# A two-layer decoder trunk on one core: weight-sum transfers tied to weight units, joined first-chunk scores, head squares summed on ScalarE, separate scrap blocks

## The chip, the cores and the metric

The kernel runs as one program on 1 core of one Trainium2 chip. The metric is the device time of one execution in microseconds (us), lower is better. TensorE (PE) multiplies matrices, VectorE (DVE) and ScalarE (ACT) work on whole tiles of 128 partitions, GpSimd (POOL) does small elementwise work and issues its own transfers, SyncE (SP) issues the other transfers.

## The reference

The input `x` is 512 tokens of 1024 numbers, float32. Two layers, each with RMS norm, one wide projection, a mixer, a gated output projection and a residual:

```python
for layer in range(DEPTH):
    h = rms_norm(x, norm_w[layer])
    y = even_layer(h, ...) if layer % 2 == 0 else hgrn2_layer(h, ...)
    x = x + y.astype(x.dtype)
```

Layer 0 splits the projected columns in two. mLSTM takes 4 heads of 128: a short convolution, then a matrix memory over chunks of 128 tokens, then `rms_norm` per head and two gates. NSA takes 8 query heads of 64 in 2 groups: q and the selected and window keys get an RMS norm per head and a partial rotation,

```python
qh = partial_rope(rms_norm(heads(q, NSA_HEADS), q_norm), pos) * (d ** -0.5)
ks_h = partial_rope(rms_norm(heads(ks, G), k_norm[1]), pos)
kw_h = partial_rope(rms_norm(heads(kw, G), k_norm[2]), pos)
```

and then come three branches of attention: over compressed blocks, over selected blocks and over a window. With 512 tokens all 8 blocks are selected and the window covers all earlier tokens, so the last two are both causal softmax attention, each with its own keys and values. Layer 1 (HGRN2) is a gated linear recurrence of 8 heads, again with `rms_norm` per head before its gate and its output projection.

## The kernel before, in words

**Products.** A float32 operand is split in a high part (`whi`, `h0h`) of TensorE's fast float32 format and the rest (`wlo`, `h0l`), and a product is three: high by high, low by high, high by low. The dense projections are groups of 96 such products of 512 columns (8 blocks of 128 inputs, 3 products, 4 banks of PSUM). The groups of layer 0 are cg, nq, nkv, nz, mq, mk, mv, mo, mz and the output o00, o01; those of layer 1 are t0 to t3 with two paired groups p0, p1 between them, and o10, o11.

**Weight units.** A group's weights come in 4 units. SP loads `raw`, ACT copies it to `whi`, DVE subtracts to get `wlo` (`cvt_w`, l. 739). `Group.convert` (l. 771) does this for a unit of the next group while the present one multiplies. There are 4 buffers each of `whi` and `wlo`.

**Weight sums.** The paired groups multiply sums of weight blocks. `sums` (in `build`) makes them in DRAM: 16 transfers issued by POOL, 12 from the weights (`wt<-in_wall_dram`) and 4 between the sums themselves (`wt<-wt`), some of them adding to their target, 1 MB each. `Adds.put` (l. 580) issues one; the strand `presums` releases number n when the planned TensorE work has passed 95 + 10.5 n us (`PS`, l. 30). The sums are first loaded for layer 1 (`raw<-wt`).

**The order of the work.** All instructions are recorded through one helper, so the profile shows them all at L408 and they are told apart by the tile names. Strands of work (Python generators) are run in turn and recorded; then `Plan.flush` (l. 392) puts every engine's instructions in an order by its own list of costs and dependences (`Plan.edges`, l. 220). Each engine then executes its list in that order and waits where an input is missing. So an edit at one place also changes the order at others.

**Head norms.** `prep_q(i)` and `prep_k(i)`, i = 0 to 3, take the projected q (8 heads of 64) and keys (4 of 64) of 128 tokens: ACT squares the whole tile into `sq`, DVE sums each head (`qss`, `kss`), POOL computes the inverse root (`qrs`, `krs`: a `TENSOR_SCALAR` and a power) and multiplies the norm's weight in (`qk<-qk,qnB`), DVE multiplies (`x<-qk,krs`) and rotates, TensorE turns the tile (`tp<-cs,x`), and ACT and DVE split it into `q` and `kd`. The mLSTM and HGRN2 head norms square one head of 128 at a time on ACT with a running sum (`accum_out`) and write the squares themselves to a scrap tile `hj` that nobody reads.

**Scores.** `nsa_a` runs 16 units (2 groups, 2 pairs of heads, 2 heads, 2 branches), each over 4 query tiles i. A unit's tile i has 128 (i+1) keys: two products of that width (high and low keys, `sc<-kd,q`), then DVE masks and takes the extreme (`nm`), ACT exponentiates into `PP` with a running sum (`sm`), DVE scales. `nsa_b` turns `PP` on TensorE (`tp<-cs,PP`) and multiplies it with the values.

Of the kernel before, what the change touches and what calls it, by code (L numbers as in the profile page):

```python
# [28 lines left out]
HBN = 4  # L29
PS = 95000.0, 10500.0  # L30
D = 1024
NT = 4
# [132 lines left out]
class Plan:  # L165
# [54 lines left out]
    def edges(self):  # L220
        for o in self.ops:
# [25 lines left out]
            if o.after is not None:  # L247
                o.pred.setdefault(o.after, 0.0)
        for a, b in zip(self.ops, self.ops[1:]):
# [323 lines left out]
class Adds:  # L573
# [3 lines left out]
    def __init__(self, plan, flow, eng):  # L577
        self.plan, self.flow, self.eng = plan, flow, eng

    def put(self, out, src, add):  # L580
        ns = 2000.0 + 128 * free_size(out) * 4 / (50.0 if add else 100.0)
        k = {"_ns": ns, "_after": next(o for o in reversed(self.plan.ops) if o.eng == "T")}
        if add:
            k["accum_op"] = OP.add
        self.flow.work("P", 1000.0)
        self.plan.add("P", self.eng.dma_start, (out, src), k, 1000.0)


# [27 lines left out]
def build(tc, I, out):  # L616
# [6 lines left out]
    with ExitStack() as ctx:  # L623
# [135 lines left out]
        class Group:  # L759
# [11 lines left out]
            def convert(self, i):  # L771
                k = self.qs[i]
                self.fetch(i + 1)
                nw = pcc("mhn", k, 2) if self.name[:2] == "o0" and k < 4 else None
                self.w[k] = cvt_w(self.raw.pop(k), self.C, nw)

            def mms(self, p, j, k):
# [152 lines left out]
        def sums(q, n):  # L930

            a, b = f"r{2 * q}", f"r{2 * q + 1}"
            t1, t2, t3, t4 = (wt[q][:, 2048 * i:2048 * (i + 1)] for i in range(4))
            steps = [(t3, wblock(b, 0), 0), (t2, wblock(a, 0), 0), (t3, wblock(b, 1), 1), (t4, wblock(a, 1), 0),
                     (t1, wblock(a, 0), 0), (t2, t3, 1), (t1, wblock(b, 0), 1), (t4, t2, 1)]
            AQ.put(*steps[n])

        A1 = {}
# [8 lines left out]
        with ExitStack() as c0:  # L947
# [3 lines left out]
            def s_t(name, shape, bufs=2, dt=F32):  # L951
                return sp.tile(shape, dt, name=name, tag=name, bufs=bufs)
# [3 lines left out]
            def hb(n):  # L956
                return lambda: big[0] >= n
# [246 lines left out]
            def turn(x2):  # L1204
# [3 lines left out]
                return cut(p, (4, 128))  # L1208

            def prep_q(i):  # L1210
                yield hb(2)
                x = qk[i][:, :8, :]
                ts_ = slice(128 * i, 128 * (i + 1))
                sq = b_t("sq", (8, 64))
                A.activation(sq, x, AF.Square)
                P.tensor_tensor(x, x, cust(qnB, [[0, 8], [1, 64]]), op=OP.mult)
                ss = s_t("qss", [128, 8])
                V.tensor_reduce(ss, sq, axis=AX.X, op=OP.add)
                b_end()
                rq = s_t("qrs", [128, 8])  # L1220
# [18 lines left out]
            def prep_k(i):  # L1239
                yield hb(2)  # L1240
                x = qk[i][:, 8:, :]
                ts_ = slice(128 * i, 128 * (i + 1))
                sq = b_t("sq", (4, 64))
                A.activation(sq, x, AF.Square)
                P.tensor_tensor(x.rearrange("p (a b) c -> p a b c", a=2), x.rearrange("p (a b) c -> p a b c", a=2),
                                cust(knB, [[64, 2], [0, 2], [1, 64]], 64), op=OP.mult)
                ss = s_t("kss4", [128, 4])
                V.tensor_reduce(ss, sq, axis=AX.X, op=OP.add)
                b_end()
                rk = s_t("krs4", [128, 4])  # L1250
# [55 lines left out]

            def nsa_a():
                yield [E("q%d" % i) for i in range(4)] + [E("k%d" % i) for i in range(4)] + [E("gt")]
                for u, (g, pr, br, hh) in enumerate(UN):
                    hg = 4 * g + 2 * pr + hh  # L1310
                    yield [hb(1), lambda u=u: ndone[0] >= u - 1, SCS]
                    pp = b_t("PP", (1280,))
                    nm = s_t("nm", [128, 4], 3)
                    sm = s_t("sm", [128, 4], 3)
                    for i in range(NT):
                        n = 128 * (i + 1)
                        yield SCS
                        s = sc_t()
                        for c in range(2):
                            T.matmul(s[:, :n], q2[g][:, hh, pr, 128 * i:128 * (i + 1)], kd[g][:, c, br, :n],  # L1320
                                     start=c == 0, stop=c == 1)
                        V.tensor_tensor_reduce(s[:, :n], s[:, :n], cz[:, 512 - n:], 1.0, -NEG, op0=OP.add, op1=OP.min,
                                               accum_out=nm[:, i:i + 1])
                        A.activation(pp[:, OFF[i]:OFF[i] + n], s[:, :n], AF.Exp, bias=nm[:, i:i + 1], scale=-1.0,
                                     accum_out=sm[:, i:i + 1])
                    V.reciprocal(sm, sm)
                    V.tensor_tensor(sm, sm, cust(gt, [[24, 4]], 3 * hg + 1 + br), op=OP.mult)
                    for i in range(NT):
                        sl = slice(OFF[i], OFF[i] + 128 * (i + 1))
                        V.tensor_scalar(pp[:, sl], pp[:, sl], sm[:, i:i + 1], None, op0=OP.mult)  # L1330
                    PPs[u] = pp
                    fl.mark(E("A%d" % u))
                    if u % 8 == 7:
                        u_end(1 + u // 8)
# [3 lines left out]
            def nsa_b():  # L1338
                pts = []
                yp = None  # L1340
                for u, (g, pr, br, hh) in enumerate(UN):
                    yield [E("A%d" % u), hb(1)]
                    pp = PPs.pop(u)
                    ptl = b_t("PT", (1280,))
                    m = []
                    for kbs, o in (((0,), 0), ((1,), 512), ((2, 3), 896)):
# [3 lines left out]
                        for kb in kbs:  # L1350
                            for i in range(kb, NT):
                                T.transpose(tp[:, c:c + 128], pp[:, OFF[i] + 128 * kb:OFF[i] + 128 * (kb + 1)], idf)
                                c += 128
# [133 lines left out]
            def m_tok(t):  # L1487
# [216 lines left out]

            def presums():

                for n in range(16):
                    yield lambda: fl.pe >= PS[0] + PS[1] * n
                    sums(n % 2, n // 2)

            fl.cur.t = 0.0
            fl.add(presums(), 0)
            fl.add(dense0(), 9)
# [4 lines left out]
        with ExitStack() as c1:  # L1718
# [60 lines left out]
            def hgrn(h):  # L1779
# [339 lines left out]
```

## Time and profile before

| | |
|---|---|
| median of 3 executions | 621.58 us (619.12 to 622.77) |
| the profiled execution | 619.54 us, its span 617.8 us |
| mean granted TensorE clock of the profiled execution | 0.997 |
| instructions | 11670 |

The profiled execution is the one that all rows below come from. The span is the time from its first to its last instruction; 1.7 us lie around it. "Busy" rows give the sum of the durations on an engine, and TensorE's products overlap, so its share of 99% counts the time in which at least one is in flight. The distance from one product's start to the next one's start is the better measure of what it costs.

### The profile page before, as it was taken

What the parts mean: (1) busy time and instruction counts of PE and PEld (TensorE: products, weight loads), DVE (VectorE), ACT (ScalarE), POOL (GpSimd) and SP (SyncE); (2) the same over time, 40 slices, a digit from 0 to 9 for tenths busy, and PEclk for the clock granted to TensorE, in tenths of its full rate; (3) what the DMA queues carried; (4) which work ended last, traced back from release to release, by engine and by line L of the source; (5) the groups of instructions that cost most, each with busy time, mean ns of one, the idle gap of its engine ahead of it and who ended that gap; (6) DMA issues with size and microseconds to landing.
All of it is one profiled execution on the core that took longest, in us unless ns stands there. A gap on an engine that the chain in (4) does not pass through costs nothing.

```text
span 617.8 us, 11670 instructions
## 1 busy us (share of the span) xinstructions
PE 609.2 (99%) x4498; PEld 492.0 (80%) x4498; DVE 463.9 (75%) x988; ACT 326.4 (53%) x778; POOL 104.5 (17%) x131
## 2 busy tenths in 40 slices
PE   8999998999999999999999999999999999999997
PEld 8877886877777777888888887788877877788886
DVE  5888989988899875656746669997688798986441
ACT  7554433675676765273534757447527375565410
POOL 1424252031100000063003111023000100122100
PEclk9998999999999999999999999999999999999999
DMA  8823137679994004016244424473222215473111
GB/s 293 278 117 103 51 103 256 203 164 342 247 203 138 0 2 147 7 46 228 77 162 136 154 85 138 118 240 121 69 72 69 70 34 173 138 282 128 35 69 68
DMA packets 23526, 82.90 MB, mean 134 GB/s; under 512 B 3376, under 2 KB 4272, under 8 KB 20656
## 3 DMA queue, kind: packets, MB, share of 16 engines
q1 hardware_dynamic: 21168, 65.39, 32.2%
q0 software_dynamic: 2304, 16.78, 10.3%
q8 instruction: 35, 0.57, 0.4%
q14 instruction: 19, 0.16, 0.1%
HBM read 77.96 MB, written 20.97 MB: 160 GB/s over the span
## 4 chain that ended last, share of the span: by engine, by line
PE 92%; DVE 3%; DMA 1%; issue 1%; POOL 1%; ACT 1%; SPq 0%; ACTq 0%; DVEq 0%
PE mm L408 35%; PE mx L408 17%; PE my L408 15%; PE sc L408 8%; PE tp L408 5%; PE ac L408 5%; PE tq L408 5%; PE sd L408 2%; DMA raw<-in_wall_dram 1%; DVE wlo L408 1%; DVE HB L408 0%; DVE AL L408 0%; POOL krs L408 0%; ACT whi L408 0%; DVE x L408 0%
## 5 line engine op out<-in xcount | busy, mean ns | idle before, releaser
L408 ACT ACTIVATE whi<-raw 128x512 fp32r<-128x512 f32 (+1 forms) x184 | 105.0, 614 | 76.2 <-PE my L408 29.5
L408 DVE TENSOR_TENSOR wlo<-raw,whi 128x1024 fp32r<-128x1024 f32 (+1 forms) x96 | 114.7, 1202 | 20.4 <-ACT whi L408 20.1
L408 PE MATMUL mm<-whi,h0h 128*128 128x512 f32 (+1 forms) x168 | 68.2, 407 | 0.0
L408 PE MATMUL mm<-whi,h0l 128*128 128x512 f32 (+1 forms) x168 | 67.9, 405 | 0.0
L408 PE MATMUL mm<-wlo,h0h 128*128 128x512 f32 (+1 forms) x168 | 67.4, 405 | 0.0
L408 ACT ACTIVATE PP<-sc,nm 128x128 f32<-128x128 f32 (+2 forms) x64 | 33.7, 527 | 26.0 <-DVE nm L408 22.9
L408 DVE CUSTOM_DVE_ANT_0 sc<-sc,cz 128x128 f32<-128x128 f32 (+2 forms) x64 | 31.4, 502 | 11.7 <-PE sc L408 9.1
L408 PE MATMUL mm<-h0h,whi 128*128 128x512 f32 x96 | 39.5, 411 | 0.0
L408 PE MATMUL mm<-h0h,wlo 128*128 128x512 f32 x96 | 38.1, 397 | 0.6 <-DVE wlo L408 0.6
L408 PE MATMUL mm<-h0l,whi 128*128 128x512 f32 x96 | 38.6, 402 | 0.0
L408 PEld LDWEIGHTS mm<-whi,h0l 128*128 128x128 f32 x168 | 32.1, 192 | 5.8 <-issue 0.2
L408 PEld LDWEIGHTS mm<-wlo,h0h 128*128 128x128 f32 x168 | 32.2, 192 | 5.6 <-issue 0.2
L408 PEld LDWEIGHTS mm<-whi,h0h 128*128 128x128 f32 x168 | 32.3, 192 | 5.2
L408 DVE TENSOR_TENSOR HB<-HB,tt 128x512 f32<-128x512 f32 x48 | 31.9, 687 | 4.4 <-PE sd L408 3.1
L408 PE MATMUL sc<-kd,q 128*128 128x512 f32 (+3 forms) x128 | 31.3, 330 | 0.0
L408 ACT ACTIVATE PT<-tp 128x384 f32<-128x384 f32 (+1 forms) x48 | 24.0, 526 | 9.5 <-PE tp L408 9.2
L408 POOL TENSOR_TENSOR ivgg<-ivgg,zz 128x256 f32<-128x256 f32 x16 | 17.8, 1116 | 65.9 <-ACT zz L408 65.9
L408 POOL TENSOR_SCALAR hr<-hs 128x4 f32<-128x4 f32 x12 | 2.3, 193 | 142.7 <-ACT hj L408 142.6
L408 PE MATMUL tp<-cs,PP 128*128 128x128 f32 x160 | 26.3, 275 | 0.0
L408 PEld LDWEIGHTS sc<-kd,q 128*128 128x128 f32 x128 | 22.7, 191 | 4.0 <-ACT PT L408 0.8
L408 PE MATMUL my<-h1l,whi 128*128 128x512 f32 x64 | 25.8, 403 | 0.0
L408 PE MATMUL mx<-h1l,whi 128*128 128x512 f32 x64 | 25.8, 402 | 0.0
(374 smaller groups left out, 1556.7 us busy)
## 6 DMA issues: line engine op xcount, KB each, us to landing
raw<-in_wall_dram SPq DMA_DIRECT2D x76, 512.0 KB, 3.8
wt<-in_wall_dram POOLq DMA_DIRECT2D x12, 1024.0 KB, 14.2
raw<-wt SPq DMA_DIRECT2D x16, 512.0 KB, 3.7
wt<-wt POOLq DMA_DIRECT2D x4, 1024.0 KB, 22.7
bias<-in_brow_dram SPq DMA_DIRECT2D x9, 256.0 KB, 4.1
xt<-in_xt_dram SPq DMA_DIRECT2D x8, 256.0 KB, 5.4
w<-in_cw_dram SPq DMA_DIRECT2D x2, 1024.0 KB, 9.4
x<-in_xt_dram SPq DMA_DIRECT2D x2, 1024.0 KB, 6.8
```

The source lines that it names most:

```text
L408: o.fn(*o.a, **k)
```

## The change

Four edits. (1) The weight-sum transfers no longer follow the strand `presums`. `Group.convert` calls `paced_sum` after 16 of the units of mq, mk, mv, mo and mz (`PACE`); it puts a small POOL instruction that reads one column of the unit's `wlo` (tile `held`) and then the next transfer behind it. (2) `squares` replaces the one wide square on ACT and the sum on DVE by one ACT square of 64 columns per head with its running sum, 8 for a q tile and 4 for a k tile. `prep_q` and `prep_k` need one of the big buffers instead of two. (3) The products of the first 128 keys of both branches are one product of 256 columns into one bank; the exponentials of branch 1's first chunk are kept in their own tile `e0` until that branch's unit runs. (4) The scrap tiles of the head norms have one block per head instead of one for all.

```diff
-PS = 95000.0, 10500.0
+PACE = {"mq": (0, 2), "mk": (0, 1, 2), "mv": (0, 1, 2), "mo": (0, 1, 2, 3), "mz": (0, 1, 2, 3)}
...
-                o.pred.setdefault(o.after, 0.0)
+                o.pred.setdefault(o.after, -o.after.k.get("_ns", 0.0))
...
-        k = {"_ns": ns, "_after": next(o for o in reversed(self.plan.ops) if o.eng == "T")}
+        k = {"_ns": ns, "_after": self.last}
...
+        self.last = self.plan.ops[-1]
...
                 self.w[k] = cvt_w(self.raw.pop(k), self.C, nw)
+                if k // 2 in PACE.get(self.name, ()):
+                    paced_sum(self.w[k][1])
...
+        held, nsum = cp.tile([128, 1], F32, name="held"), [0]
+
+        def paced_sum(lo):
+
+            keep, n = fl.cur.t, nsum[0]
+            P.tensor_scalar(held, lo[:, :1].bitcast(F32), 1.0, None, op0=OP.mult, _after=AQ.last)
+            AQ.last = pl.ops[-1]
+            sums(n % 2, n // 2)
+            fl.cur.t, nsum[0] = keep, n + 1
...
+            def squares(x, ss):
+
+                j = cut(s_t("sqj", [128, 512], 1), (8, 64))
+                for a in range(x.shape[1]):
+                    A.activation(j[:, a, :], x[:, a, :], AF.Square, accum_out=ss[:, a:a + 1])
+
             def prep_q(i):
-                yield hb(2)
+                yield hb(1)
...
-                sq = b_t("sq", (8, 64))
-                A.activation(sq, x, AF.Square)
+                ss = s_t("qss", [128, 8])
+                squares(x, ss)
                 P.tensor_tensor(x, x, cust(qnB, [[0, 8], [1, 64]]), op=OP.mult)
-                ss = s_t("qss", [128, 8])
-                V.tensor_reduce(ss, sq, axis=AX.X, op=OP.add)
-                b_end()
...
+                    if br == 0:
+                        for b_ in range(2):
+                            mm_[b_, hh] = s_t(f"nm{b_}", [128, 4], 3), s_t(f"sm{b_}", [128, 4], 3)
+                        first[hh] = s_t("e0", [128, 128], 3)
+                    nm, sm = mm_[br, hh]
...
-                    for i in range(NT):
+                    for i in range(br, NT):
...
-                            T.matmul(s[:, :n], q2[g][:, hh, pr, 128 * i:128 * (i + 1)], kd[g][:, c, br, :n],
-                                     start=c == 0, stop=c == 1)
...
+                            T.matmul(s[:, :n] if i else cut(s, (2, 128)), q2[g][:, hh, pr, 128 * i:128 * (i + 1)],
+                                     kd[g][:, c, br, :n] if i else kd[g][:, c, :, :n], start=c == 0, stop=c == 1)
+                        chunk(s[:, :n], n, i, pp[:, OFF[i]:OFF[i] + n], nm, sm)
+                        if i == 0:
+                            chunk(s[:, 128:256], n, i, first[hh], *mm_[1, hh])
...
-                hj = s_t("hj", [128, 128], 1)
+                hj = cut(s_t("sqj", [128, 512], 1), (4, 128))
                 for h in range(4):
-                    A.activation(hj, nd[:, h, :128], AF.Square, scale=rd[:, h:h + 1], accum_out=hs[:, h:h + 1])
+                    A.activation(hj[:, h, :], nd[:, h, :128], AF.Square, scale=rd[:, h:h + 1], accum_out=hs[:, h:h + 1])
...
-                hj = s_t("hj1", [128, 128], 1)
+                hj = s_t("hj1", [128, 4, 128], 1)
                 for t in range(4):
-                    A.activation(hj, op[:, 128 * t:128 * (t + 1)], AF.Square, accum_out=hs[:, t:t + 1])
+                    A.activation(hj[:, t, :], op[:, 128 * t:128 * (t + 1)], AF.Square, accum_out=hs[:, t:t + 1])
```

`prep_k` changes as `prep_q` does. In `nsa_a`, `chunk` holds the mask and exponential that stood in the loop, and `nsa_b` turns `e0` (as `p0`) in place of the first chunk of `PP`.

The edits also move instructions. The rows below are each engine's list, one row per instruction (xN: N in a row), `out<-in` and the shape written.

ScalarE's list at the first two q tiles, before (`gb` belongs to the mLSTM gates, `kn` to the compressed keys, `whi` to the next weights, `q_202` and `q_203` are the split q):

```order
L408 ACTIVATE sq<-qk 128x512
L408 ACT_TABLE_LOAD
L408 ACTIVATE gb<-gb 128x128
L408 ACTIVATE whi<-raw 128x512 x2
L408 ACTIVATE gb<-tp 128x64
L408 ACTIVATE sq<-qk 128x512
L408 ACTIVATE kn,kss<-kr 64x64
L408 ACTIVATE whi<-raw 128x512 x2
```

The same place after the change:

```order
L408 ACTIVATE sqj,qss<-qk 128x64 x16
L408 ACT_TABLE_LOAD
L408 ACTIVATE gb<-gb 128x128
L408 ACTIVATE gb<-tp 128x64
L408 ACTIVATE whi<-raw 128x512 x4
L408 ACTIVATE kn,kss<-kr 64x64
L408 ACTIVATE whi<-raw 128x512 x2
L408 ACTIVATE q_203<-tp 64x2x128
L408 ACTIVATE q_204<-tp 64x2x128
L408 ACTIVATE q_203<-tp 64x2x128
L408 ACTIVATE sqj,qss<-qk 128x64 x8
```

The squares of the second tile have moved ahead of the table load, and both tiles together are 16 instructions in a row.

GpSimd's list at the last three k tiles, before (`krs` is the inverse root, `knB` the norm's weight, `th` a part of the mLSTM convolution):

```order
L408 TENSOR_SCALAR krs_246<-kss_245 128x4
L408 TENSOR_TENSOR krs_246<-krs_246,hm 128x4
L408 TENSOR_SCALAR krs_263<-kss_262 128x4
L408 TENSOR_TENSOR krs_263<-krs_263,hm 128x4
L408 TENSOR_TENSOR qk<-qk,knB 128x256
L408 DMA wt_71<-in_wall_dram 128x2048
L408 TENSOR_TENSOR qk<-qk,knB 128x256
L408 TENSOR_SCALAR krs_271<-kss_270 128x4
L408 TENSOR_TENSOR krs_271<-krs_271,hm 128x4
L408 DMA wt_72<-in_wall_dram 128x2048
L408 TENSOR_SCALAR th<-th 128x512
L408 DMA wt_71<-in_wall_dram 128x2048
```

And after:

```order
L408 TENSOR_SCALAR krs_248<-kss_246 128x4
L408 TENSOR_TENSOR qk<-qk,knB 128x256
L408 TENSOR_TENSOR krs_248<-krs_248,hm 128x4
L408 TENSOR_SCALAR krs_267<-kss_265 128x4
L408 TENSOR_TENSOR qk<-qk,knB 128x256
L408 TENSOR_TENSOR krs_267<-krs_267,hm 128x4
L408 TENSOR_SCALAR krs_275<-kss_273 128x4
L408 TENSOR_TENSOR krs_275<-krs_275,hm 128x4
L408 TENSOR_TENSOR qk<-qk,knB 128x256
L408 TENSOR_SCALAR th<-th 128x512 x2
L408 TENSOR_SCALAR held<-wlo 128x1
L408 DMA wt_71<-in_wall_dram 128x2048
```

No transfer stands among the k tiles any more; the first one follows the second `th` row and its `held`. Of the 16, twelve stand between there and the first `hr` row of the mLSTM head norms, and four between the rows of these norms, where before there was none.

TensorE's list at the first scores, before (`ce` belongs to the compressed branch, `mm` are the products of a dense group):

```order
L408 MATMUL mm<-h0h,whi 128x512
L408 MATMUL mm<-h0l,whi 128x512
L408 MATMUL sc<-kd,q_202 128x128
L408 MATMUL tp<-cs,ce 128x128
L408 MATMUL sc<-kd,q_202 128x128
L408 MATMUL tp<-cs,ce 128x128
L408 MATMUL sc<-kd,q_202 128x256 x2
L408 MATMUL mm<-h0h,wlo 128x512
```

And after:

```order
L408 MATMUL tp<-cs,ce 128x128 x2
L408 MATMUL mm<-h0l,whi 128x512
L408 MATMUL mm<-h0h,wlo 128x512
L408 MATMUL sc<-kd,q_203 128x256 x4
L408 MATMUL mm<-h0h,whi 128x512
L408 MATMUL mm<-h0l,whi 128x512
L408 MATMUL mm<-h0h,wlo 128x512
L408 MATMUL mm<-h0h,whi 128x512
L408 MATMUL tp<-cs,x_276 128x128 x4
```

Two of the four 256-wide products are the joined first chunks, and the scores now start ahead of the turn of a last k tile (`tp<-cs,x`). Over the whole program the 32 products `sc<-kd,q` of 128 columns are gone and those of 256 have gone from 32 to 48; all else that TensorE does is kept in number.

## Rows read from the trace of the kernel before

**Rows 1.** The page: busy time of each engine with its share of the span and its instructions, and the chain of work that ended last, followed back, by engine.

```profile
PE 609.2 (99%) x4498; PEld 492.0 (80%) x4498; DVE 463.9 (75%) x988; ACT 326.4 (53%) x778; POOL 104.5 (17%) x131
...
PE 92%; DVE 3%; DMA 1%; issue 1%; POOL 1%; ACT 1%; SPq 0%; ACTq 0%; DVEq 0%
```

**Rows 2.** Stretches of the span: start and end in us, length, busy time with instructions in brackets of PE, weight load, DVE, ACT and POOL, then the granted clock as a share of full speed, the DMA engines' busy share and GB/s.

```profile
36.00:96.00 60.00, 58.09 (x336) 46.53 (x334) 51.30 (x119) 23.78 (x54) 25.57 (x28) 0.97 0.27 86
50.00:54.00 4.00, 4.00 (x12) 3.15 (x13) 3.37 (x10) 0.34 (x1) 0.00 (x0) 0.57 0.09 14
100.00:150.00 50.00, 50.00 (x266) 39.31 (x264) 43.98 (x125) 32.95 (x84) 9.48 (x15) 1.00 0.73 225
```

**Rows 3.** The timeline of PE at two places with score products: start us, duration us, engine, line, operation, names, shapes, count.

```profile
110.65 0.33 PE L408 MATMUL sc<-kd,q 128*128 128x128 f32 x2
...
111.11 0.39 PE L408 MATMUL mm<-h0h,wlo 128*128 128x512 f32 x1
111.34 0.39 PE L408 MATMUL mm<-h0h,whi 128*128 128x512 f32 x1
...
122.65 0.40 PE L408 MATMUL sc<-kd,q 128*128 128x256 f32 x2
122.89 0.40 PE L408 MATMUL mm<-h0h,wlo 128*128 128x512 f32 x1
```

**Rows 4.** The timeline of PE from 93 to 96 us; in square brackets the idle time before an instruction and what ended it.

```profile
93.07 0.39 PE L408 MATMUL mm<-h0l,whi 128*128 128x512 f32 x1
94.05 0.50 PE L408 MATMUL mm<-h0h,wlo 128*128 128x512 f32 x1 [0.59 <-DVE wlo L408]
94.39 0.39 PE L408 MATMUL mm<-h0h,whi 128*128 128x512 f32 x1
95.99 0.63 PE L408 MATMUL tp<-cs,x 128*128 128x128 f32 x4 [1.21 <-DVE kd L408]
```

**Rows 5.** The timeline of DVE over the same time.

```profile
91.40 0.69 DVE L408 TENSOR_TENSOR x<-qk,krs 128x512 f32<-128x512 f32 x1 [1.48 <-POOL qk L408]
92.01 1.98 DVE L408 TENSOR_TENSOR wlo<-raw,whi 128x1024 fp32r<-128x1024 f32 x1
93.92 0.41 DVE L408 TENSOR_REDUCE kss<-sq 128x4 f32<-128x256 f32 x1
...
95.09 0.75 DVE L408 TENSOR_TENSOR kd<-tp,kd 128x256 fp32r<-128x256 f32 x2
```

**Rows 6.** The timeline of POOL ahead of it.

```profile
88.36 1.22 POOL L408 TENSOR_SCALAR krs<-kss 128x4 f32<-128x4 f32 x1 [6.25 <-DVE kss L408]
...
91.31 0.81 POOL L408 DMA_DIRECT2D wt<-in_wall_dram  x1
```

**Rows 7.** Groups of instructions by line and shape: names, shapes, count, then busy us in total, mean ns of one, and the idle time before them with what ended most of it.

```profile
L408 ACT ACTIVATE sq<-qk 128x512 f32<-128x512 f32 x4 | 2.5, 628 | 2.5 <-DVE qk L408 2.5
L408 ACT ACTIVATE sq<-qk 128x256 f32<-128x256 f32 x4 | 1.7, 416 | 3.6 <-DVE qk L408 3.5
...
L408 DVE TENSOR_REDUCE qss<-sq 128x8 f32<-128x512 f32 x4 | 2.7, 675 | 0.0
```

**Rows 8.** The timeline of ACT at four places.

```profile
37.97 1.28 ACT L408 ACT_TABLE_LOAD   x1
...
42.50 0.31 ACT L408 ACTIVATE gb<-gb 128x128 f32<-128x128 f32 x1 [3.25 <-DVE gb L408]
...
47.65 0.26 ACT L408 ACTIVATE kn<-kr 64x64 f32<-64x64 f32 x1 [1.20 <-DVE kr L408]
47.82 0.19 ACT L408 ACTIVATION_READ_ACCUMULATOR kn<-kr 64x1 f32 x1
...
263.98 0.19 ACT L408 ACTIVATION_READ_ACCUMULATOR hj<-nd,rd 128x1 f32 x1
264.07 0.61 ACT L408 ACTIVATE gz<-gz 128x512 f32<-128x512 f32 x1
```

**Rows 9.** The timeline of ACT in a head norm of layer 1.

```profile
493.68 0.28 ACT L408 ACTIVATE hj<-tq 128x128 f32<-128x128 f32 x1 [3.86 <-PE tq L408]
...
494.08 0.28 ACT L408 ACTIVATE hj<-tq 128x128 f32<-128x128 f32 x1
```

**Rows 10.** The timeline of PE behind that head norm, and behind one of the last.

```profile
496.48 0.39 PE L408 MATMUL my<-h1h,whi 128*128 128x512 f32 x1
497.06 0.33 PE L408 MATMUL tq<-cs,yo 128*128 128x128 f32 x1 [0.20 <-DVE yo L408]
...
585.10 0.40 PE L408 MATMUL my<-y1l,whi 128*128 128x512 f32 x1
585.64 0.30 PE L408 MATMUL tq<-cs,yo 128*128 128x128 f32 x1
```

**Rows 11.** Everything on the tile `wt`: operation and count, shortest, median and longest duration in ns, first and last start in us; then the time from issue to landing.

```profile
L408 SPq DMA_DIRECT2D raw<-wt x16: 319/319/327, 370.2 to 535.4; - x16
L408 POOL DMA_DIRECT2D wt<-in_wall_dram x12: 523/848/1466, 91.3 to 154.1; - x12
...
DMA to landing us min/median/max: 3.3/5.3/26.1
```

**Rows 12.** The mLSTM head norms: one row of POOL's timeline, and the products on PE that read their result (durations in ns, first and last start).

```profile
280.82 2.06 POOL L408 TENSOR_TENSOR nd<-nd,gz 128x512 f32<-128x512 f32 x1
...
L408 PE MATMUL mm<-ymh,whi x28: 391/397/398, 313.9 to 346.3; 128*128 128x512 f32 x28
```

More of the change, by code (lines that the diff above doesn't have):

```diff
@@ L577, in __init__ @@
     def __init__(self, plan, flow, eng):
-        self.plan, self.flow, self.eng = plan, flow, eng
+        self.plan, self.flow, self.eng, self.last = plan, flow, eng, None
     def put(self, out, src, add):
         ns = 2000.0 + 128 * free_size(out) * 4 / (50.0 if add else 100.0)
-        k = {"_ns": ns, "_after": next(o for o in reversed(self.plan.ops) if o.eng == "T")}
+        k = {"_ns": ns, "_after": self.last}
         if add:
@@ L1239, in prep_k @@
             def prep_k(i):
-                yield hb(2)
+                yield hb(1)
                 x = qk[i][:, 8:, :]
                 ts_ = slice(128 * i, 128 * (i + 1))
-                sq = b_t("sq", (4, 64))
-                A.activation(sq, x, AF.Square)
+                ss = s_t("kss4", [128, 4])
+                squares(x, ss)
                 P.tensor_tensor(x.rearrange("p (a b) c -> p a b c", a=2), x.rearrange("p (a b) c -> p a b c", a=2),
                                 cust(knB, [[64, 2], [0, 2], [1, 64]], 64), op=OP.mult)
-                ss = s_t("kss4", [128, 4])
-                V.tensor_reduce(ss, sq, axis=AX.X, op=OP.add)
-                b_end()
                 rk = s_t("krs4", [128, 4])
@@ L1307, in nsa_a @@
             def nsa_a():
+                mm_, first = {}, {}
                 yield [E("q%d" % i) for i in range(4)] + [E("k%d" % i) for i in range(4)] + [E("gt")]
@@ L1312, in nsa_a, with chunk @@
                     pp = b_t("PP", (1280,))
-                    nm = s_t("nm", [128, 4], 3)
-                    sm = s_t("sm", [128, 4], 3)
-                    for i in range(NT):
+                    if br == 0:
[3 more added lines that the diff above has]
+                    nm, sm = mm_[br, hh]
+                    def chunk(s, n, i, p, nm, sm):
+                        V.tensor_tensor_reduce(s, s, cz[:, 512 - n:], 1.0, -NEG, op0=OP.add, op1=OP.min,
+                                               accum_out=nm[:, i:i + 1])
+                        A.activation(p, s, AF.Exp, bias=nm[:, i:i + 1], scale=-1.0, accum_out=sm[:, i:i + 1])
+                    for i in range(br, NT):
                         n = 128 * (i + 1)
@@ L1319, in nsa_a @@
                         for c in range(2):
-                            T.matmul(s[:, :n], q2[g][:, hh, pr, 128 * i:128 * (i + 1)], kd[g][:, c, br, :n],
-                                     start=c == 0, stop=c == 1)
[L1322 to L1325, printed above, removed]
+                            T.matmul(s[:, :n] if i else cut(s, (2, 128)), q2[g][:, hh, pr, 128 * i:128 * (i + 1)],
[3 more added lines that the diff above has]
+                            chunk(s[:, 128:256], n, i, first[hh], *mm_[1, hh])
                     V.reciprocal(sm, sm)
@@ L1328, in nsa_a @@
                     for i in range(NT):
-                        sl = slice(OFF[i], OFF[i] + 128 * (i + 1))
-                        V.tensor_scalar(pp[:, sl], pp[:, sl], sm[:, i:i + 1], None, op0=OP.mult)
-                    PPs[u] = pp
+                        ps = pp[:, OFF[i]:OFF[i] + 128 * (i + 1)] if i or br == 0 else first[hh]
+                        V.tensor_scalar(ps, ps, sm[:, i:i + 1], None, op0=OP.mult)
+                    PPs[u] = pp, first[hh] if br else pp[:, :128]
                     fl.mark(E("A%d" % u))
@@ L1342, in nsa_b @@
                     yield [E("A%d" % u), hb(1)]
-                    pp = PPs.pop(u)
+                    pp, p0 = PPs.pop(u)
                     ptl = b_t("PT", (1280,))
@@ L1351, in nsa_b @@
                             for i in range(kb, NT):
-                                T.transpose(tp[:, c:c + 128], pp[:, OFF[i] + 128 * kb:OFF[i] + 128 * (kb + 1)], idf)
+                                src = pp[:, OFF[i] + 128 * kb:OFF[i] + 128 * (kb + 1)] if i else p0
+                                T.transpose(tp[:, c:c + 128], src, idf)
                                 c += 128
@@ L1703, in dense0 @@
                 u_end(4)
[L1705 to L1709, printed above, removed]
             fl.cur.t = 0.0
-            fl.add(presums(), 0)
             fl.add(dense0(), 9)
```

## The prediction

> **What bounds the kernel now.** I read the page's busy line and chain first, then the stretches, then single places of the timeline. The reader is to see that TensorE has a product in flight for 609.2 of 617.8 us, 99%, and that the chain that ended last is PE for 92% [rows 1]. So time can go in three ways only: fewer columns on PE, less waiting by PE, or a higher clock. How much PE waits is read from stretches. From 100 to 150 us it is busy 50.00 of 50.00 us, although the transfers of the weight sums run there at a DMA share of 0.73 [rows 2]. From 36 to 96 us it is busy 58.09 of 60 [rows 2], and the timeline has the two places where this is lost: a product of a dense group that waits for its `wlo` from DVE, and the turn of a k tile that waits for DVE's `kd` [rows 4]. The third loss is clock: from 50 to 54 us the granted clock is 0.57 of full speed on average, a mix of the 1.2 and the 2.4 GHz level, with PE busy all the time [rows 2].
>
> **The joined first chunks.** Sixteen pairs of 128 columns go and eight pairs of 256 come; nothing else on PE changes in number. A dense product costs 0.23 us, start to start (111.11 to 111.34). A pair of 128 and one dense product take 110.65 to 111.11, 0.46 us, so the pair costs 0.23 too. A pair of 256 takes 122.65 to 122.89, 0.24 us [rows 3]. So a pair costs nearly the same at half the width: 16 x 0.23 - 8 x 0.24 = 3.68 - 1.92 = 1.76 us. PE is busy throughout there, so all of it counts: **-1.7**.
>
> **The wait at 93 to 96 us.** Start to start, 93.07 to 94.05 is 0.98 and 94.39 to 95.99 is 1.60 [rows 4]; less 0.23 each, PE loses 0.75 + 1.37 = 2.1 us. Followed back: DVE waited 1.48 us for POOL's `qk` and started `x` only at 91.40, then `wlo` took 1.98 us, then came a sum of squares of 0.41 and the rotation, then `kd` at 95.09 [rows 5]. On POOL the `TENSOR_SCALAR` of the first of these k tiles took 1.22 us, and the issue of a weight-sum transfer took it 0.81 us from 91.31, among them [rows 6]. After the change the transfers stand behind the k tiles, the sum of squares is no DVE instruction any more (four of 0.675 us and four of 0.41, 4.3 us of DVE [rows 5, 7]), and the scores start ahead of the last k turn, so that turn has other work in front of it. All of this points one way, but the order of this stretch is new, and what was late once can be late elsewhere. Between 0 and -2.1 I take **-1.3**.
>
> **The small squares.** A square of 64 columns with its sum is an `ACTIVATE`, 0.17 us later its accumulator read (47.65 to 47.82), and ACT's next instruction starts 0.09 us behind that read's start (263.98 to 264.07) [rows 8]: 0.26 us each if nothing waits. 48 x 0.26 = 12.5 us stand for 4 x 0.628 + 4 x 0.416 = 4.2 us [rows 7]: ACT gets 8.3 us more, in a stretch where it is busy 23.78 of 60 us and DVE 51.30 [rows 2]. The cover is ACT's idle 36 us; what isn't covered is the queue behind a row of squares. The first row is 16 long. It starts one wide square (0.63) ahead of the table load at 37.97, so at 37.3, and ends at 41.5; with the load (1.28) `gb` starts at about 42.8 in place of 42.50 [rows 7, 8]. Each later row holds up conversions of weights (`whi`) and q splits behind it by 8 x 0.26 - 0.63 = 1.45 us (q) or 4 x 0.26 - 0.42 = 0.6 us (k). Bounds are 0 and +8.3; as there is four times the needed idle time I stay near the lower end, half of one q row: **+0.7**.
>
> On fixed costs per instruction, the trace shows 0.26 us for 64 columns. The Trainium skill (ScalarE: Activation LUTs, section "What ACT_TABLE_LOAD costs") gives 186 ns plus 0.833 ns per column, with neighbours overlapping by 93 ns: estimated from that page, 0.146 us each and 7.0 us for 48, so only +2.8 us of ACT and a term of some +0.2. The page's figure has no accumulator read in it, and the row has; the row decides.
>
> **The scrap blocks.** In a head norm of layer 1 the squares start 0.40 us apart (493.68 to 494.08) [rows 9], against 0.26 where the next instruction does not write the same scrap [rows 8]. Three gaps of 0.14 give 0.42 us less per head norm. PE sees it only where it waits for the norm's end: at 496.48 to 497.06 it loses 0.35 us on `yo`, and at 585.10 to 585.64 another 0.31 [rows 10]. Bounds 0 and -0.7; I take **-0.5**.
>
> **The transfers.** They start between 91.3 and 154.1 us [rows 11]. Moving them gains nothing behind 100 us, since PE doesn't wait there [rows 2]. Their new cost is 16 small POOL rows, and a wait: each `held` waits for its unit's `wlo`, and queued behind it on POOL are the transfer, the `th` rows and, at the end, the mLSTM head norms. The sums are first loaded at 370.2 us [rows 11]. The last transfer is issued ahead of the fourth and last norm, about 290 us, as the third one's multiplication ran at 280.82 [rows 12]; the longest landing was 26.1 us [rows 11], so some 54 us are to spare. Four transfers of 0.85 us [rows 11] and four `held` add about 4.5 us to POOL between the norms, and from 282.9 PE has 31 us until it reads their result (`ymh`, 313.9) [rows 12]. With that cover I count **0**; without it, it is the rival below.
>
> **The sum.** -1.7 - 1.3 - 0.5 + 0.7 = -2.8 us against the profiled execution's own 619.54 us: 616.7. That execution is 2.04 us under the median of the runs, 621.58; against the median I predict 618.8 us. A difference of 0.5%, 3.1 us, is about what can be told from no change here.
>
> **The rivals.**
> - *More goes than I count.* The whole wait of 2.1 and 0.7 for the scrap blocks, 1.7 for the products, and the slow-clock stretch too: 4.00 us at 0.57 is the work of 2.3 us, 1.7 lost [rows 2]. The order ahead of 50 us is new, so PE may be fed well enough to keep its clock. 1.7 + 2.1 + 0.7 + 1.7 = 6.2: 613.3 of its own, 615.4 against the median. Against it: no row says that the squares are what PE lacks ahead of it. Chance 0.18.
> - *The small squares become the bound* (slower). Place: 37 to 96 us, where every q and k tile's inverse root now waits for 8 or 4 ACT instructions in a row, and the next weights' `whi` wait in the same queue. Price: up to 8.3 us exposed in place of 0.7. With -3.5 for the rest it is slower than before from 3.5 us exposed, and measurably so from 6.6; all 8.3 give 619.54 + 4.8 = 624.3, or 626.4 against the median. For it: DVE and POOL wait for this chain already (POOL 6.25 us for `kss` [rows 6]). Against it: ACT is idle 60% of the stretch. Chance 0.14.
> - *`held` holds up weights or norms* (slower). Place: 264 to 288 us, where POOL has multiplications of up to 2.06 us [rows 12] between the transfers. A `wlo` buffer is free only when its `held` has run, and POOL takes its list in order. A unit of 12 products for each of 2 input blocks lasts 24 x 0.23 = 5.5 us on PE; a hold by three multiplications and a transfer, 3 x 2.06 + 0.85 = 7.0 us, would exceed it by 1.5, four times 6.0 us: sum +3.2, 624.8 against the median. It decides once a hold passes the lead of the conversions; there are four buffers, which speaks against. Chance 0.08.
> - *Nothing but the products.* The wait at 93 us only moves, and what the scrap saves is waited for elsewhere: -1.7 + 0.7 = -1.0, 620.6. That the transfers were never in the way is part of this. Chance 0.15.
>
> **How the numbers follow.** The forecast has 0.45, with a range of its own of 617 to 620.5 from its terms' bounds and a spread of 1 us between medians. Faster by over 0.5% (under 618.5): 0.22 of the forecast's 0.45, all of the first rival, a little of the last: 0.41. Slower by over 0.5% (over 624.7): most of the two slower rivals, 0.15. Within: 0.44. The range goes from 614.8, just under the first rival, to 622.8, which leaves most of the slower ones out, some 2 in 10 in all.
>
> **What would show it.** The scores' rows: 48 products of 256 and none of 128. At the turn of the last k tiles PE without a bracketed wait of over 0.5 us. Squares on ACT 0.26 us apart, and `hj` 0.26 in place of 0.40. `gb` at about 42.8 us. No wait of PE for `wlo` or `ymh` between 264 and 315 us, nor of `raw<-wt` behind its landing. Wrong it is if PE's waits for `whi`, `wlo`, `q` or `kd` between 37 and 110 us add up to more than the 2.1 us of before, or if the clock row falls in a second place.

## The result and the profile after

| | before | after |
|---|---|---|
| median | 620.84 us (619.12 to 622.77, 6 executions) | 616.90 us (615.52 to 617.95, 6 executions) |
| profiled execution | 619.54 us, span 617.8 | 615.52 us, span 613.7 |
| granted clock of the profiled execution | 0.997 | 1.000 |

The ratio of after to before is 0.9948 (95% interval 0.993 to 0.9967): 0.5% faster, 3.2 us by this ratio and 3.9 by the two medians, just past what I had called distinguishable. The prediction was 618.8 us, range 614.8 to 622.8. Two executions far off all others, one of the kernel before at 664.84 us and one of e7 at 3371.21, are left out of the ratios and means below.

The page of the changed kernel, its busy line and its chain, answers to [rows 1]:

```profile
PE 603.9 (98%) x4482; PEld 487.5 (79%) x4482; DVE 456.0 (74%) x980; ACT 329.3 (54%) x866; POOL 109.9 (18%) x147
...
PE 87%; DVE 6%; POOL 2%; issue 2%; DMA 1%; ACT 1%; SPq 0%; DVEq 0%; POOLq 0%; ACTq 0%
```

PE still bounds it. Sixteen products fewer, 5.3 us less in flight; the chain now passes through DVE and POOL for longer.

Two stretches of the changed kernel, columns as in [rows 2]:

```profile
36.00:96.00 60.00, 58.82 (x349) 47.36 (x348) 50.46 (x129) 32.69 (x144) 24.24 (x26) 1.00 0.25 77
50.00:54.00 4.00, 4.00 (x17) 3.12 (x18) 2.11 (x6) 1.19 (x5) 1.42 (x2) 1.00 0.83 239
```

ACT's load rose by 8.9 us, about as worked out, and PE is busy 0.7 us longer in the same 60 us. The granted clock is 1.00 at 50 to 54 us, where it was 0.57.

The waits of PE, by engine and tile waited for: us in all, times, longest:

```profile
PE sc L408 <- ACT whi L408: 2.0, 2, 1.3
PE ac L408 <- POOL hm L408: 1.0, 1, 1.0
PE tq L408 <- ACT kT L408: 0.9, 1, 0.9
PE tp L408 <- DVE kd L408: 0.8, 1, 0.8
PE tp L408 <- DVE nd L408: 0.7, 1, 0.7
```

The first two lie at the start of the program. The waits of [rows 4] are gone; the 0.8 for `kd` stands at another place, at a turn of the compressed branch:

```profile
85.55 0.28 PE L408 MATMUL sc<-kcd,q 128*128 128x64 f32 x1
86.61 0.30 PE L408 MATMUL tp<-cs,ce 128*128 128x128 f32 x1 [0.79 <-DVE kd L408]
```

Two more are new: for `nd`, the mLSTM head norm, and for `kT` in layer 1.

The new wait for `nd` in the timeline of PE:

```profile
286.81 0.40 PE L408 MATMUL mm<-whi,h0l 128*128 128x512 f32 x1
287.94 0.66 PE L408 MATMUL tp<-cs,nd 128*128 128x128 f32 x4 [0.73 <-DVE nd L408]
```

From start to start 1.13 us, so 0.9 lost.

The little squares and the scrap blocks in the timeline of ACT; the last two rows answer to [rows 9]:

```profile
37.49 0.24 ACT L408 ACTIVATE sqj<-qk 128x64 f32<-128x64 f32 x1
37.64 0.19 ACT L408 ACTIVATION_READ_ACCUMULATOR sqj<-qk 128x1 f32 x1
37.73 0.24 ACT L408 ACTIVATE sqj<-qk 128x64 f32<-128x64 f32 x1
...
488.52 0.28 ACT L408 ACTIVATE hj<-tq 128x128 f32<-128x128 f32 x1 [3.38 <-PE tq L408]
...
488.79 0.27 ACT L408 ACTIVATE hj<-tq 128x128 f32<-128x128 f32 x1
```

A little square costs 0.24 us (0.26 predicted), and a head norm's squares start 0.27 us apart instead of 0.40.

**Where the time went.** All kernels here run the same 1896 dense products with the output names `mm`, `mx` and `my`, so the n-th one's start can be set against the n-th of another trace. Number 48 lies ahead of the changed part, 600 behind the last scores, 768 behind the mLSTM norms.

| dense product | 48 | 600 | 768 | 1895 |
|---|---|---|---|---|
| before | 26.90 | 239.88 | 296.35 | 614.04 |
| after | 26.58 | 235.16 | 292.49 | 609.99 |

From 48 to 600 the changed kernel gains 212.98 - 208.58 = 4.4 us, from 600 to 768 it loses 0.9, and behind that it gains 0.2. Of the 4.4, 0.9 is no matter of the lists: e3 and e11 below have the list of before on PE in this stretch, and their profiled executions, without the slow clock at 50 to 54 us, take 212.10 and 212.07.

### The profile page after: what moved, and what is told of

It reads as the page before. It is cut to its first block, busy times and chain, and to the rows that moved or that the text cites. A ratio compares the mean times of both kernels' runs of the same rounds, so it can differ in the third digit from the quotient of the medians.

```text
span 613.7 us, 11758 instructions
## 1 busy us (share of the span) xinstructions
PE 603.9 (98%) x4482; PEld 487.5 (79%) x4482; DVE 456.0 (74%) x980; ACT 329.3 (54%) x866; POOL 109.9 (18%) x147
## 4 chain that ended last, share of the span: by engine, by line
PE 87%; DVE 6%; POOL 2%; issue 2%; DMA 1%; ACT 1%; SPq 0%; DVEq 0%; POOLq 0%; ACTq 0%
PE mm L408 31%; PE mx L408 17%; PE my L408 15%; PE sc L408 7%; PE tp L408 5%; PE ac L408 5%; PE tq L408 5%; PE sd L408 2%; DVE wlo L408 2%; DMA xt<-in_xt_dram 1%; POOL hr L408 1%; DVE ivgg L408 1%; DVE HB L408 1%; DMA raw<-in_wall_dram 1%; DVE AL L408 0%
## 5 line engine op out<-in xcount | busy, mean ns | idle before, releaser
L408 ACT ACTIVATE PP<-sc,nm 128x256 f32<-128x256 f32 (+3 forms) x56 | 30.8, 551 | 26.6 <-DVE nm L408 25.8
L408 DVE CUSTOM_DVE_ANT_0 sc<-sc,cz 128x512 f32<-128x512 f32 (+3 forms) x64 | 31.1, 503 | 12.2 <-PE sc L408 9.3
L408 PE MATMUL mm<-h0h,whi 128*128 128x512 f32 x96 | 38.0, 399 | 0.0
L408 POOL TENSOR_TENSOR ivgg<-ivgg,zz 128x256 f32<-128x256 f32 x16 | 16.2, 1012 | 68.5 <-ACT zz L408 68.5
L408 PE MATMUL sc<-kd,q 128*128 128x256 f32 (+2 forms) x112 | 28.4, 345 | 0.0
L408 POOL TENSOR_SCALAR held<-wlo 128x1 f32<-128x1 f32 x16 | 6.1, 383 | 115.8 <-DVE wlo L408 94.0
L408 PE MATMUL my<-h1h,whi 128*128 128x512 f32 x64 | 25.8, 403 | 0.0
L408 PE MATMUL mx<-h1h,whi 128*128 128x512 f32 x64 | 25.7, 402 | 0.0
```

The source lines that it names most:

```text
L408: o.fn(*o.a, **k)
```

## The experiments

The first four each make one edit alone, on the kernel before. The ratios to the kernel before are told with their 95% intervals.

**e1, joined first chunks only** (`nsa_a` and `nsa_b` as in the change).

```diff
-                            T.matmul(s[:, :n], q2[g][:, hh, pr, 128 * i:128 * (i + 1)], kd[g][:, c, br, :n],
+                            T.matmul(s[:, :n] if i else cut(s, (2, 128)), q2[g][:, hh, pr, 128 * i:128 * (i + 1)],
+                                     kd[g][:, c, br, :n] if i else kd[g][:, c, :, :n], start=c == 0, stop=c == 1)
```

> The kernel before with only the joined first-chunk products. Theory of terms: PE has 32 products of 128 columns less and 16 of 256 more, worth -1.7 us wherever they stand; the dense product number 576 (behind the last scores) starts 1.7 us earlier than in the kernel before, and the waits at 93 to 96 us and the slow clock at 50 to 54 us stay as they are, as the products stand behind them: ratio 0.997. Rival, order: the edit moves hundreds of rows on PE and DVE, so waits of up to 2 us go or come elsewhere between 36 and 250 us; then number 576 is off from -1.7 by more than 1 us either way.

620.38 us, ratio 1.0001 (0.9985 to 1.0016): no gain. Its profiled execution had the slow clock at another place, in the stretch 94 to 108 us:

```profile
94.00:108.00 14.00, 12.32 (x54) 9.88 (x55) 12.79 (x37) 4.34 (x11) 2.94 (x5) 0.88 0.74 258
50.00:54.00 4.00, 4.00 (x19) 2.79 (x19) 3.16 (x11) 1.34 (x4) 0.00 (x0) 1.00 0.01 4
```

0.88 over 14 us is 1.7 us lost. Without it 48 to 600 would take an estimated 213.32 - 1.7 = 211.6, about 0.5 less than e3 and e11, not 1.7.

**e2, small squares only** (`squares`, `prep_q` and `prep_k` as in the change).

```diff
-                sq = b_t("sq", (8, 64))
-                A.activation(sq, x, AF.Square)
+                ss = s_t("qss", [128, 8])
+                squares(x, ss)
```

> The kernel before with only the small squares on ScalarE. Theory of terms: 8.3 us more on ACT at most half a row exposed (+0.7), 4.3 us less on DVE, of which PE sees only the shorter wait at 93 to 96 us (-0.3 to -0.8): about 0, ratio 0.999 to 1.001. Rival, squares cure: the wait at 93 to 96 us and the slow clock at 50 to 54 us go with this edit alone: -2.1 and -1.7, ratio 0.994. Rival, bound: PE waits for whi, q or kd for over 3 us in all between 37 and 110 us: ratio over 1.004.

624.30 us, ratio 1.0059 (1.0036 to 1.0083): slower by 3.7 us. By the number it looks like the rival in which the squares become the bound, but the trace names another place: no such sum of waits in 37 to 110 us, and one wait of 3.5 us for `PP` at 155 us:

```profile
155.01 0.40 PE L408 MATMUL mm<-h0h,whi 128*128 128x512 f32 x1
158.94 0.80 PE L408 MATMUL sc<-kd,q 128*128 128x256 f32 x2 [3.53 <-ACT PP L408]
```

The squares don't cure the slow clock either: from 50 to 54 us it is 0.71 here, and 0.57 in e6 below. ACT stood for the 6.6 us up to 153.73, waiting for a weight load:

```profile
153.73 1.15 ACT L408 ACTIVATE whi<-raw 128x512 fp32r<-128x512 f32 x2 [6.59 <-DMA raw<-in_wall_dram]
```

**e3, scrap blocks only.**

```diff
-                hj = s_t("hj1", [128, 128], 1)
+                hj = s_t("hj1", [128, 4, 128], 1)
...
-                    A.activation(hj, op[:, 128 * t:128 * (t + 1)], AF.Square, accum_out=hs[:, t:t + 1])
+                    A.activation(hj[:, t, :], op[:, 128 * t:128 * (t + 1)], AF.Square, accum_out=hs[:, t:t + 1])
```

(and the same for the mLSTM norm)

> The kernel before with only the separate scrap blocks. Theory of terms: squares of a head 0.26 us apart instead of 0.40, head norm 0.42 us shorter; PE's two waits for yo (0.35 and 0.30 us) go: -0.5 us, ratio 0.999. Nothing ahead of 425 us changes. Rival, order: the list of PE in layer 1 changes at some 24 rows, and with it the waits on sd at 456 and 460 us (0.4 and 0.3 us) go too: -1.2 to -1.4 us. Rival, nothing: what is saved is waited for at the next step: 0.

619.35 us, ratio 0.9977 (0.9961 to 0.9993): -1.4 us, with -0.4 inside the interval. Among executions with a granted clock of 0.9985 or more the means are 619.06 (9) and 619.69 (37, before): -0.6.

**e4, transfers tied to weight units only.**

```diff
+                if k // 2 in PACE.get(self.name, ()):
+                    paced_sum(self.w[k][1])
...
-            fl.add(presums(), 0)
```

> The kernel before with only the transfers tied to weight units. Theory of terms: the wait at 93 to 96 us shortens by the issue of 0.8 us on POOL and what POOL lost beside it (-0.8 to -2.1), and the fourth mLSTM head norm comes later by its transfers' issues, so that PE waits for nd at about 290 us for 0.9 us: sum 0 to -1.2, ratio 0.998 to 1.0. Rival, contention: transfers at 91 to 167 us slowed POOL, DVE and the weight loads all along; then PE gains over 1 us between 100 and 250 us. Rival, order: number 576 moves by what neither says.

621.43 us, ratio 1.0018 (1.0002 to 1.0034): slower by 1.1. The wait at 93 to 96 us stays (1.2 us for `kd`, 0.3 for `wlo`), 48 to 600 takes 211.75, 0.3 less than e3 and e11, and the turn of the head norm loses more than in the changed kernel, 1.4 us. With that, 600 to 768 takes 57.91 instead of the 56.45 of e3; less the 0.3 it is the 1.1:

```profile
290.34 0.40 PE L408 MATMUL mm<-whi,h0l 128*128 128x512 f32 x1
292.01 0.66 PE L408 MATMUL tp<-cs,nd 128*128 128x128 f32 x4 [1.28 <-DVE nd L408]
```

By these ratios the single edits are worth 0, +3.7, -1.4 and +1.1 us, and all four together -3.2. They don't add up. The next four start from the changed kernel.

**e5, no transfer between the head norms.**

```diff
-PACE = {"mq": (0, 2), "mk": (0, 1, 2), "mv": (0, 1, 2), "mo": (0, 1, 2, 3), "mz": (0, 1, 2, 3)}
+PACE = {"mq": (0, 1, 2, 3), "mk": (0, 1, 2, 3), "mv": (0, 1, 2, 3), "mo": (0, 1, 2, 3)}
```

> The changed kernel with the 16 transfers behind the units of mq, mk, mv and mo, all four of each, none behind mz. The lists of PE, ACT and SP stay as they are; on POOL the last four transfers and their held rows stand ahead of the first head norm instead of between the norms. Theory that the wait of PE for nd at 286.8 us comes from these transfers: it goes, PE's 0.9 us come back, 0.9 us less than the changed kernel. Rival: the wait comes from the norm's own chain and stays. The sums are read at 366 us, and the last landing would be near 260 us, so nothing is late.

616.77 us, ratio 0.9944 (0.9931 to 0.9957). PE's turn no longer waits:

```profile
287.24 0.39 PE L408 MATMUL mm<-whi,h0l 128*128 128x512 f32 x1
287.46 0.60 PE L408 MATMUL tp<-cs,nd 128*128 128x128 f32 x4
```

600 to 768 takes 56.40 us instead of 57.32: the 0.9 is back, so the transfers between the norms are its cause. In the changed kernel POOL had a transfer's issue between the two rows of the fourth norm's inverse root; in e5 they stand next to each other. First the changed kernel, then e5:

```profile
281.70 0.19 POOL L408 TENSOR_SCALAR hr<-hs 128x4 f32<-128x4 f32 x1 [0.71 <-ACT sqj L408]
282.14 0.88 POOL L408 DMA_DIRECT2D wt<-wt  x1 [0.24 <-issue]
282.74 1.37 POOL L408 TENSOR_TENSOR hr<-hr,hm 128x4 f32<-128x4 f32 x1
```

```profile
281.08 0.19 POOL L408 TENSOR_SCALAR hr<-hs 128x4 f32<-128x4 f32 x1 [2.07 <-ACT sqj L408]
281.35 1.01 POOL L408 TENSOR_TENSOR hr<-hr,hm 128x4 f32<-128x4 f32 x1
```

In the whole time it doesn't show: e5's profiled execution lost 1.7 us more than the changed kernel's behind product 768, with the same list on PE. In layer 1 two executions with the same list on PE differ by more than this term.

**e6, without the joined first chunks** (`nsa_a` and `nsa_b` as before).

```diff
-                            T.matmul(s[:, :n] if i else cut(s, (2, 128)), q2[g][:, hh, pr, 128 * i:128 * (i + 1)],
-                                     kd[g][:, c, br, :n] if i else kd[g][:, c, :, :n], start=c == 0, stop=c == 1)
+                            T.matmul(s[:, :n], q2[g][:, hh, pr, 128 * i:128 * (i + 1)], kd[g][:, c, br, :n],
```

> The changed kernel without the joined first chunks (the 32 products of 128 columns are back). Theory of terms: 1.7 us slower than the changed kernel, waits unchanged: ratio to before 0.997 to 0.998. Rival, order: waits of over 1 us come or go.

619.94 us, ratio 0.999 (0.9972 to 1.0008): 3 us slower than the changed kernel, where 1.7 was expected. The rival has part in it: PE waits 1.1 us for `x` and 1.1 for `vp` ahead of 100 us, where the changed kernel waits 0.8 for `kd` and 0.2 for `kcd`.

**e7, without the small squares** (`prep_q` and `prep_k` as before).

```diff
-                squares(x, ss)
+                A.activation(sq, x, AF.Square)
...
+                V.tensor_reduce(ss, sq, axis=AX.X, op=OP.add)
```

> The changed kernel with the wide squares and the sums on DVE. Theory of terms: ACT 8.3 us less, DVE 4.3 us more; PE's waits between 37 and 110 us grow by under 1 us: within 1 us of the changed kernel. Rival, squares cure: the slow clock at 50 to 54 us and a wait of some 2 us near 94 us are back: 2 to 4 us slower than the changed kernel.

619.92 us, ratio 1.0002 (0.9986 to 1.0018): 3 us slower than the changed kernel. The timeline of PE has the wait at 93 to 96 us of [rows 4] again, nearly as before:

```profile
92.81 0.40 PE L408 MATMUL mm<-h0l,whi 128*128 128x512 f32 x1
93.60 0.50 PE L408 MATMUL mm<-h0h,wlo 128*128 128x512 f32 x1 [0.39 <-DVE wlo L408]
93.94 0.39 PE L408 MATMUL mm<-h0h,whi 128*128 128x512 f32 x1
95.53 0.63 PE L408 MATMUL tp<-cs,x 128*128 128x128 f32 x4 [1.21 <-DVE kd L408]
```

The first transfer is issued at 108.6 us in e7. So that wait comes and goes with the squares edit, not with the transfers among the k tiles. Whether DVE's sums make it, or the order that this edit changes, was not separated. The slow clock of the rival is not back: from 50 to 54 us it is 1.00.

**e8, without the tied transfers** (`PS`, `presums`, `Adds` and `edges` as before).

```diff
-                if k // 2 in PACE.get(self.name, ()):
-                    paced_sum(self.w[k][1])
...
+            fl.add(presums(), 0)
```

> The changed kernel with the transfers released by the strand again. Theory of terms: PE's wait for nd at 286.8 us goes (-0.9), and a transfer's issue on POOL stands among the k tiles again (0 to +2.1): -0.9 to +1.2 against the changed kernel. Rival, contention: over 1 us lost between 100 and 250 us.

623.09 us, ratio 1.0053 (1.004 to 1.0066): 6 us slower than the changed kernel, far outside the -0.9 to +1.2 of the terms. The rival had named such a loss, without its size. PE, ACT, and then the stretch behind on PE:

```profile
143.69 0.99 PE L408 MATMUL sc<-kd,q 128*128 128x384 f32 x4
150.06 0.90 PE L408 MATMUL tp<-cs,PP 128*128 128x128 f32 x3 [5.38 <-ACT PT L408]
```

```profile
148.89 0.63 ACT L408 ACTIVATE whi<-raw 128x512 fp32r<-128x512 f32 x1 [6.92 <-DMA raw<-in_wall_dram]
149.43 0.96 ACT L408 ACTIVATE PT<-tp 128x512 f32<-128x512 f32 x2
```

```profile
150.00:154.00 4.00, 3.94 (x11) 3.27 (x12) 1.24 (x4) 3.74 (x10) 0.82 (x1) 0.50 1.02 250
```

ACT takes its list in order, and a weight load that isn't there holds up the copy `PT` that PE waits for. Behind the wait PE runs at half the full clock, the 1.2 GHz level, for these 4 us: another 2 us. e2 has the same chain of waits. The transfers from 100 to 170 us in e8, by issue: size of one and median us to landing:

```profile
wt<-in_wall_dram POOLq DMA_DIRECT2D x10, 1024.0 KB, 21.8
raw<-in_wall_dram SPq DMA_DIRECT2D x8, 512.0 KB, 11.4
```

The weight loads take 11.4 us to land. In the changed kernel's same stretch it is 6.2, beside five transfers of sums instead of fourteen; in the kernel before it is 7.5. The last four test this: the lists of all engines as they are, but each weight-sum transfer moves 1/16 of its columns.

```diff
-        self.plan.add("P", self.eng.dma_start, (out, src), k, 1000.0)
+        self.plan.add("P", lambda o, i, **q: self.eng.dma_start(o[:, :128], i[:, :128], **q), (out, src), k, 1000.0)
...
+        real = self.wall[:, :1024] if src.tensor.name[:2] == "wt" else src
+        self.plan.add("Q", lambda o, i: self.eng.dma_start(o, real), (out, src), {"_ns": n * 4 / 360.0}, 475.0)
```

**e9, e8 with small transfers.**

> The changed kernel with the strand's transfers (e8), all engines' lists as in e8, but each weight-sum transfer moves 128 of its 2048 columns, and layer 1 loads its paired weights from the given weights instead of the sums (so its output is not the reference's). Theory that the 1 MB transfers hold up SP's weight loads, and ACT, waiting 6.9 us for one of them, holds up PE: the loads land in about 4 us, ACT's and PE's waits near 144 us go, 5 to 6 us less than e8: 616 to 618 us. Rival, order or issue: PE's wait of 5.4 us near 144 us stays, as POOL and ACT have the same lists.

617.35 us, ratio 0.9945 (0.9927 to 0.9963). The waits are gone, on ACT and on PE, and the loads land in 3.6 us:

```profile
raw<-in_wall_dram SPq DMA_DIRECT2D x8, 512.0 KB, 3.6
wt<-in_wall_dram POOLq DMA_DIRECT2D x10, 64.0 KB, 4.1
```

From 48 to 600: 216.31 us in e8, 208.76 in e9, 208.58 in the changed kernel. That the bytes of the transfers do it, and not their place on POOL, is shown.

**e10, e2 with small transfers.**

> The kernel before with only the small squares (e2), transfers of 128 columns as in e9 (output of layer 1 not the reference's). Theory: the 3.7 us that PE loses at 155 us go, and what is left is the cost of the small squares by themselves: the waits for x at 66 and 99 us (1.3 and 1.2 us) in place of the waits at 93 to 96 us (2.1 us): 0 to +0.5 us against the kernel before. Rival, bound: the squares by themselves cost 3 us or more, then it stays near 624 us.

620.38 us, ratio 0.9995 (0.9979 to 1.0012): by themselves the small squares cost and gain nothing that can be measured. PE's waits at 93 to 96 us are replaced by two in front of turns of `x`:

```profile
65.80 0.33 PE L408 MATMUL tp<-cs,x 128*128 128x128 f32 x1 [1.12 <-DVE x L408]
...
98.40 0.33 PE L408 MATMUL tp<-cs,x 128*128 128x128 f32 x1 [1.07 <-ACT vp L408]
```

**e11, before with small transfers.**

> The kernel before, transfers of 128 columns as in e9 (output of layer 1 not the reference's). Theory, as predicted: PE does not wait for anything that the transfers hold up in this list, so the time stays within 0.5 us of the kernel before. Rival: transfers cost it something everywhere (weight loads, POOL issues among the k tiles): 1 to 3 us less.

620.13 us, ratio 0.9995 (0.9977 to 1.0012): the transfers cost the kernel before nothing that can be measured.

**e12, after with small transfers.**

> The changed kernel, transfers of 128 columns as in e9 (output of layer 1 not the reference's). Theory: paced transfers hold up no weight load, so nothing changes but PE's wait for nd at 287 us, which stays if the issue on POOL takes as long for a small transfer (0.9 us) and shrinks if it is shorter: 0 to -0.9 us against the changed kernel. Rival: paced transfers still cost weight loads: over 1 us less.

616.64 us, ratio 0.9934 (0.991 to 0.9957): 0.3 us from the changed kernel, no difference. The wait for `nd` stays at 0.7 us: the 16 issues take POOL 0.85 us each in the median, as with large transfers (0.84).

## Why the prediction was right, and where its steps were not

The forecast, slightly faster, held: 2.8 us were forecast and 3.2 measured by the ratio. The time lay in the range, 1.9 us under the number; 0.7 of that is the median of before, 620.84 with six executions and 621.58 with three. That the sum came out so near is partly luck, as costs and gains that it left out stand against each other. The steps:

- **Joined chunks, -1.7.** The products themselves save what was worked out. From each start to PE's next start, idle time left out, the score products take 22.19 us in e4 and 20.19 in e7 (wide squares), 22.21 in e10 and 20.42 in e9 (small ones): 2.0 and 1.8 less. What the step had wrong is that this is all that counts. The 160 turns of the exponentials (`tp<-cs,PP`, with `tp<-cs,e` for `e0`) take 1.2 and 0.9 us more: fewer of them stand right ahead of a score product (22 to 9, and 21 to 12), where PE's next start follows 0.04 to 0.06 us later, and more ahead of another turn, where it follows after 0.11. And PE's idle time goes up by 0.35 us with wide squares and down by 1.1 with small ones. In all, 48 to 600 falls from 211.75 to 211.28, by 0.5, with wide squares. With small ones it falls from 213.03 to 208.76, by 4.3, of which 1.7 is the work of eleven mLSTM products that e10 has in this stretch and e9 behind it (48 to 768 falls from 267.73 to 265.20), leaving 2.5. The mean, 1.5, is near the term by luck; it holds in neither list.
- **The wait at 93 to 96 us, -1.3 between 0 and -2.1.** It went, 2.1, and 0.95 (for `kd` at 85.5 us) and 0.3 came at other places, a net of about -0.9. Of the causes that I named, the squares edit is shown (e7 has the wait without a transfer, e10 lost it with the transfers' issues in place), though not whether DVE's sums or the new order do it; the transfer's issue on POOL is worth little: with e4 alone the wait shrinks by 0.3 us.
- **Small squares, +0.7.** 0 in e10, with the gain of the step above inside: PE has two other waits there, 2.2 us together, which are gone in the changed kernel. What part the squares have in them was not tried. The cost per square came out at 0.24; the row of 16 ran from 37.00 to 41.1 us, and `gb` started at 42.38 (42.8 expected).
- **Scrap blocks, -0.5.** -0.6 by executions at full clock, -1.4 by medians. The wait for `yo` at 497 us is down from 0.35 to 0.2 and the one at 585 us is gone.
- **Transfers, 0.** This step failed twice. First, "from 282.9 PE has 31 us until it reads their result": PE reads the norms earlier, where it turns `nd` at 287.9, and in that list the norm was just in time. The rival named the place (264 to 288 us) but not this way, by transfers issued between the norms' own POOL rows; it cost 0.9 us (e5). Second, "moving them gains nothing behind 100 us, since PE doesn't wait there": true of the list of before (e11), false of the new one. With the small squares ACT comes to a weight unit's copy before its load has landed when the strand's transfers are in the way (6.6 us in e2, 6.9 in e8); with the joined chunks alone it waits 1.6 us there (e1), and PE not at all. In the changed kernel's list tying them to the weight units is worth 6 us (e8, e9). The sum had neither this loss of the small squares nor its cure, so it doesn't show there. I had read a row of no waits as if it held for any order of the work.
- **The slow clock** I put in a rival alone. In 37 of 81 executions the kernel before has a granted clock of 0.9985 or more and a mean of 619.69 us; 33 have 0.996 or 0.997 and 620.72, 11 have 0.991 to 0.995 and 623.25. So the loss comes in several sizes; the 1.7 us of [rows 2] is one stretch, and 48 to 600 is only 0.9 longer with it than in e11. The changed kernel had 3 executions of 6 at 0.9985 or more, with 616.10, and the others 617.51. Like for like at the full clock the gain is 3.6 us. What I counted on the profiled execution's 619.54 as "its own time" had this loss in it and the profiled one after had not, which makes up part of the 4.0 us between the two.
- Unforeseen: PE's wait for `kT` near 551 us, about 1 us. It is there in all kernels with joined chunks (0.7 to 1.4) and under 0.4 or absent in those without. Why an edit of layer 0 makes it was not tried.

## What to carry to other kernels

Where a planner orders the work, an edit's price holds for the list it was measured in: single edits of 0, +3.7, -1.4 and +1.1 us made -3.2 together, because each one opens or closes a wait of another. A stretch without waits says that background transfers are hidden now, not that they stay hidden when an in-order engine gets to its loads sooner; look at the landing times of the loads (7.5 us here against 3.5 without the transfers) rather than at the waits. And when work is put on a queue, follow its results to their first reader, whichever instruction that is.

## What the runs showed of the hardware

- A transfer's issue on POOL is no shorter for a small one: 0.85 us in the median with 64 KB (e12) and 0.84 with 1 MB (the changed kernel), and the wait that it causes stays at 0.7 us.
- ACT squares of 64 columns with a running sum come every 0.24 us, accumulator read included, if each writes its own scrap; writing the same scrap puts the next one some 0.14 us later (128 columns, before against e3: 0.40 and 0.25 in layer 1, 0.53 and 0.39 in the mLSTM norms).
- The slow clock comes and goes with the same list on PE: at 50 to 54 us the granted clock is 0.57 in the kernel before and 1.00 in e11, and from 46 to 50 us PE was busy 4.00 of 4.00 us in both. Behind the wait of 5.4 us in e8 it is 0.50, and all 5 executions of e8 have a granted clock of 0.992 to 0.995 over the whole. In e9, without that wait, the profiled execution has 1.00, 4 of 11 have 0.999 or more, and the others 0.994 to 0.997.
